# Conditioning sums taken one block of 512 at a time on TensorE or VectorE, with six half tiles instead of four

## The chip, the cores and the metric

The kernel runs on one core of a Trainium2 chip. The metric is the time of one launch on the device, in microseconds (us). A launch is one pass through a two-layer model with 256 latent tokens and 256 context tokens.

## The reference, cut to what matters

Each layer makes six vectors of 1024 values (shift, scale and gate, twice) from a conditioning vector and a 1024 x 6144 matrix. They are used wherever the layer is normalised or its result is added:

```
cond_lat = silu(c)                      # 1 x 1024
cond_ctx = silu(c_ctx)                  # 1024
for layer in range(2):
    sh1, sc1, g1, sh2, sc2, g2 = split(cond_lat @ ada_w[layer] + ada_b[layer], 6)
    h_l = rmsnorm(x, norm1_g[layer]) * (1 + sc1) + sh1
    if layer == 0:                      # the context rows need shift and scale once
        csh1, csc1, ... = split(cond_ctx @ ada_w[0] + ada_b[0], 6)
        y = hybrid_mix(h_c, h_l, ...)   # SSD heads and latent attention heads
    else:
        y = chunk_gmlp(h_l, ...)
    x = x + g1 * y
    x = x + g2 * peer(rmsnorm(x, norm2_g[layer]) * (1 + sc2) + sh2, ...)
return rmsnorm(x, final_norm_g)
```

So `cond @ ada_w` is a product of one row (two, where the context needs them) with 2 x 1024 x 6144 numbers of 4 bytes.

## The kernel before, in words

**Stages.** `hybrid` (layer 0's mixer) runs first, then `peer(0)`, `gmlp`, and `peer(1)`. In the profile `hybrid` lasts until about 440 us; its scheduled part, in which the change lies, until about 392 us.

**How the order is made.** The kernel keeps a model of the engines' clocks (`Clock`, `Engine`): every call to an engine (`T` for TensorE, `V` for VectorE, `S` for ScalarE, `G` for GpSimd, `Q` for the SP queue's transfers) adds an assumed cost to that engine's clock. `schedule` takes several generators (streams) and steps, each time, the one whose engine's clock is earliest, unless the condition it last yielded is not yet true. Out of this comes one fixed order of instructions per engine; on the chip every engine runs its own list in that order and waits on semaphores where data or a buffer is not there. All recorded operations carry line 173, the line of the helper that issues them, so that the tile names tell them apart. A matmul with an output of 32 partitions is assumed to cost 0.45 us, whatever stands next to it.

**The conditioning rows.** `ada_w` is cut into six groups of 2048 columns (two layers, three groups each); a group is four blocks of 512 sums. Layer 0's first group is made by `ada_first` and `second`, which the change leaves as they are. The other five, 20 blocks of 512 sums, are made by the stream `adas`, one after the other, through `ada_group`. In a group, block `t` (0 to 3) is accumulated over eight 128-row pieces `k` into the partitions 32t to 32t+31 of one PSUM bank. Each of the 160 pieces is a tile `aw` of 128 x 512 numbers (256 KB) that is loaded by the SP queue and then multiplied with `condT[:, k, :]` (128 x 32, of which two columns are not zero):

```
units = [(k, t) for k in range(KD) for t in range(4)]
mm(ps[32 * t:32 * t + 32, :], condT[:, k, :], bufs[i % n + j], k == 0, k == KD - 1)
```

`k` is the outer loop, `t` the inner, so that neighbouring matmuls write to different 32-partition column groups of the bank. Loads and matmuls go in pairs: a pair of tiles is loaded again when both have been used. There are four tiles (`NAW = 4`). When a group is complete, VectorE adds the bias to the whole bank (`ada_tail`).

**What stands beside it.** `adas` shares `schedule` first with the input products (`products`: tiles `whl`, `hh`, `hl`), the convolution (`conv`: `cacc`, `xch`), `dkv`, `decays`, `xtrans`, `cqs` and `states`, and then with the heads (`scores`: `kn`, `qn`, `krT`, `pe`; `values`: `pT`, `vt`; `segments`, `weights`, `outputs`: `seg`, `MT`, `yt`) and `joined` (`w_out`). The weights of those products are loaded by the same SP queue into four tiles `wr`, rounded by ScalarE into one half of three tiles `whl`, and the rest, their difference, is put by GpSimd (or VectorE) into the other half.

Of the kernel before, what the change touches and what calls it, by code (L numbers as in the profile page):

```python
# [17 lines left out]
ALU = mybir.AluOpType  # L18
AX = mybir.AxisListType

P = 128
D = 1024
KD = 8
# [26 lines left out]
EARLIER = 2.5  # L50
RUSH, SPREAD = 5.0, 2.6
PACE = 1.0
NAW = 4
KORDER = (8, 10, 12, 0, 2, 4, 6, 14)
LATE = 6.0
LAG = 2
# [151 lines left out]
def tile_backbone(ctx: ExitStack, tc: tile.TileContext, a: dict, out: bass.AP):  # L208
# [3 lines left out]
    clock = Clock()  # L212
    clk = clock.at
    T, V, S, G, Q = (Engine(e, n, clock) for e, n in ((nc.tensor, "T"), (nc.vector, "V"), (nc.scalar, "S"), (nc.gpsimd, "G"), (nc.sync, "D")))
# [28 lines left out]
    class Banks:  # L243
# [5 lines left out]
        def get(self):  # L249
            self.free.sort(key=clock.idle)  # L250
            return self.free.pop(0)
# [4 lines left out]
    def at(*aps):  # L256

        return lambda: clk["T"] + SLACK >= max(clock.ready(x) for x in aps)

    def mm(o, lhsT, rhs, start=True, stop=True):  # L260
        if rhs.dtype == F32 and lhsT.dtype == F32 and len(rhs.shape) == 2 and rhs.shape[1] == 512 and o.shape[0] == P:

            T.matmul(o[:, :256], lhsT, rhs[:, :256], start=start, stop=False)
            T.matmul(o[:, 256:], lhsT, rhs[:, 256:], start=False, stop=stop)
            return
        T.matmul(o, lhsT, rhs, start=start, stop=stop)
# [14 lines left out]
    ones = cp.tile([P, P], F32, name="ones")  # L281
# [24 lines left out]
    condT = cp.tile([P, KD, 32], F32, name="condT")  # L306
# [199 lines left out]
    def ada_tail(m, ps):  # L506
        V.tensor_tensor(m, ps, m, op=ALU.add)

    def ada_group(l, g, get, bufs, ps):

        units = [(k, t) for k in range(KD) for t in range(4)]
        n = len(bufs)
        for i in range(0, len(units) + n, 2):
            if i >= n:

                yield at(*bufs[i % n:i % n + 2])
                for j in range(2):
                    k, t = units[i - n + j]
                    mm(ps[32 * t:32 * t + 32, :], condT[:, k, :], bufs[i % n + j], k == 0, k == KD - 1)
            if i < len(units):  # L520
                yield lambda: clk["T"] >= max(clock.idle(x) for x in bufs[i % n:i % n + 2])
                for j in range(2):
                    k, t = units[i + j]
                    Q.dma_start(out=bufs[i % n + j], in_=a["ada_w"][l, k * P:(k + 1) * P, g * 2048 + t * 512:g * 2048 + (t + 1) * 512])
        ada_tail(get(), ps)
        yield

# [86 lines left out]
    def hybrid(mod):  # L614
# [87 lines left out]
        xw = e3.enter_context(tc.tile_pool(name="xw", bufs=1, side="right"))  # L702
        awb = [(ha if i < 3 else xw).tile([P, 512], F32, name=f"aw{i}") for i in range(NAW)]

# [39 lines left out]
        def adas():  # L744

            yield lambda: "mod1" in done
            ps = B.get()
            for l, g in ((0, 1), (0, 2), (1, 0), (1, 1), (1, 2)):
                if l == 0:
                    mod.append(mod_load(0, g))  # L750
                    yield from ada_group(l, g, lambda: mod[g], awb, ps)
                    done.add(("mod", g))
                    if g == 2:
                        mod2(0, mod, awb[0])
                elif g == 0:
                    yield from ada_group(l, g, lambda: nmod.append(mod_load(1, 0)) or nmod[0], awb, ps)
                else:
                    mt = ha.tile([P, 512], F32, name="mt", tag="mt")
                    yield from ada_group(l, g, lambda: mod_load(1, g, mt), awb, ps)
                    if g == 2:  # L760
                        mod2(1, [None, None, mt], awb[0])
                    S.dma_start(out=ms[g - 1], in_=mt)
            B.put(ps)
# [1410 lines left out]
```

## Time and profile before

| | |
|---|---|
| median of 3 runs | 1991.39 us (1984.33 to 1993.25) |
| the profiled execution: its time | 1996.46 us |
| the profiled execution: span of its instructions | 1994.7 us |
| mean granted TensorE clock in it | 0.97 of full speed |
| TensorE busy | 1863.6 us, 93% |
| VectorE busy | 1369.0 us, 69% |
| GpSimd busy | 629.5 us, 32% |
| ScalarE busy | 540.2 us, 27% |
| conditioning tiles loaded as `aw` | 164, of 256 KB each |

The page's busy time of TensorE counts the modelled run of each matmul through the array, and matmuls of one engine may overlap. A float32 matmul leaves two records in the trace, so that "x8" in a row on such matmuls means four of them. The idle time of an engine is given with what ended it. Of the rest of the page only what the rows below show is needed.

### The profile page before, as it was taken

What the parts mean: (1) busy time and instruction counts of PE and PEld (TensorE: products, weight loads), DVE (VectorE), ACT (ScalarE), POOL (GpSimd) and SP (SyncE); (2) the same over time, 40 slices, a digit from 0 to 9 for tenths busy, and PEclk for the clock granted to TensorE, in tenths of its full rate; (3) what the DMA queues carried; (4) which work ended last, traced back from release to release, by engine and by line L of the source; (5) the groups of instructions that cost most, each with busy time, mean ns of one, the idle gap of its engine ahead of it and who ended that gap; (6) DMA issues with size and microseconds to landing.
All of it is one profiled execution on the core that took longest, in us unless ns stands there. A gap on an engine that the chain in (4) does not pass through costs nothing. (4 is left out here: it accounts for less than half of the span.)

```text
span 1994.7 us, 27972 instructions
## 1 busy us (share of the span) xinstructions
PE 1863.6 (93%) x9888; PEld 1539.0 (77%) x9888; DVE 1369.0 (69%) x3376; ACT 540.2 (27%) x1428; POOL 629.5 (32%) x400
## 2 busy tenths in 40 slices
PE   7989999899999999998999698999999999989994
PEld 4666565679988878887878588799888888868773
DVE  4466276546985898778567625479858986876667
ACT  5334344345212222110111354442112221111111
POOL 2324312276010222133322198650112221334222
PEclk9999999899999999999999899999999999989998
DMA  8656766155367989699999474453579885999993
GB/s 314 217 173 220 251 219 212 68 180 169 128 218 276 358 301 365 221 359 367 398 417 395 149 254 147 161 188 128 195 286 362 302 342 220 355 355 400 417 411 128
DMA packets 133064, 529.87 MB, mean 266 GB/s; under 512 B 17941, under 2 KB 18133, under 8 KB 105197
## 3 DMA queue, kind: packets, MB, share of 16 engines
q1 hardware_dynamic: 97440, 301.76, 42.8%
q0 software_dynamic: 34176, 225.07, 28.9%
q8 instruction: 78, 1.28, 0.3%
q10 hardware_dynamic: 1296, 1.16, 0.2%
q14 instruction: 74, 0.61, 0.1%
HBM read 540.28 MB, written 6.91 MB: 274 GB/s over the span
## 5 line engine op out<-in xcount | busy, mean ns | idle before, releaser
L173 POOL DMA_INDIRECT rows<-in_uv,gidx x224 | 270.4, 1207 | 912.9 <-DVE acc L173 657.5
L173 PE MATMUL pb<-wr,ge 128*128 128x256 f32 x2400 | 539.5, 384 | 19.5 <-DMA wr<-in_dn 17.5
L173 PE MATMUL pa<-phf,wr 128*128 128x256 f32 x2400 | 539.1, 385 | 0.0
L173 PEld LDWEIGHTS pb<-wr,ge 128*128 128x128 f32 x2400 | 453.7, 191 | 103.1 <-DMA wr<-in_dn 41.9
L173 PEld LDWEIGHTS pa<-phf,wr 128*128 128x128 f32 x2400 | 458.9, 193 | 61.8
L173 POOL TENSOR_TENSOR whl<-wr,whl 128x1024 fp32r<-128x1024 f32 (+2 forms) x128 | 310.6, 2440 | 306.6 <-ACT whl L173 298.9
L173 DVE SCALAR_TENSOR_TENSOR junk<-rows,h 128x1024 bf16<-128x1024 f32 x224 | 273.8, 1222 | 128.7 <-DMA rows<-in_uv,gidx 128.6
L173 DVE SCALAR_TENSOR_TENSOR acc<-rows,wt,acc 128x1024 f32<-128x1024 f32 x220 | 281.8, 1281 | 0.3 <-ACT wt L173 0.3
L173 ACT ACTIVATE act<-act 128x1 f32<-128x1 f32 x230 | 46.7, 203 | 573.7 <-DVE junk L173 554.8
L173 ACT CAST whl<-wr 128x1024 fp32r<-128x1024 f32 (+2 forms) x136 | 137.3, 1019 | 86.3 <-PE pa L173 37.2
L173 ACT ACTIVATE sg<-pa 128x8 f32<-128x8 f32 (+20 forms) x98 | 26.5, 270 | 278.1 <-PE pa L173 252.3
L173 PE MATMUL pb<-oc,o 128*128 128x75 f16 x1024 | 85.3, 252 | 14.8 <-DVE oc L173 13.6
L173 PE MATMUL pa<-phh,whl 128*128 128x256 f32 x512 | 96.3, 285 | 2.2 <-DVE phf L173 1.5
L173 PEld LDWEIGHTS <-o 128*128 128x128 f16 x1024 | 78.0, 118 | 24.0 <-DVE oc L173 14.8
L173 ACT ACTIVATE ge<-pa 128x256 f32<-128x256 f32 (+18 forms) x146 | 46.9, 321 | 144.9 <-PE pa L173 144.3
L173 PE MATMUL pa<-aw,condT 128*32 128x512 f32 x320 | 78.7, 605 | 6.9 <-DMA aw<-in_ada_w 5.1
L173 PEld LDWEIGHTS pa<-phh,whl 128*128 128x128 f32 x512 | 80.7, 191 | 3.6 <-DVE phf L173 1.9
L173 DVE SCALAR_TENSOR_TENSOR ge<-pb,ge 128x292 f32<-128x292 f32 (+19 forms) x128 | 42.1, 370 | 59.4 <-ACT ge L173 56.5
L173 PE MATMUL pa<-phl,whl 128*128 128x256 f32 x256 | 73.2, 286 | 2.4 <-POOL phl L173 1.3
L173 DVE TENSOR_TENSOR o<-iotaJ,pkT 128x1024 f16<-128x1024 f16 x64 | 43.8, 684 | 36.8 <-PE pb L173 36.8
L173 ACT ACTIVATE wt<-act,gsel 128x1 f32<-128x1 f32 x224 | 66.0, 295 | 7.3
L173 DVE MAX8 ge<-ge 128x8 f32<-128x128 f32 (+1 forms) x192 | 38.4, 254 | 26.0 <-ACT ge L173 25.9
(490 smaller groups left out, 2436.6 us busy)
## 6 DMA issues: line engine op xcount, KB each, us to landing
wr<-in_dn SPq DMA_DIRECT2D x300, 512.0 KB
aw<-in_ada_w SPq DMA_DIRECT2D x164, 256.0 KB
wr<-in_wq SPq DMA_DIRECT2D x32, 512.0 KB
wr<-in_w_out SPq DMA_DIRECT2D x16, 512.0 KB
wr<-in_gm_w_v SPq DMA_DIRECT2D x16, 512.0 KB
wr<-in_gm_w_u SPq DMA_DIRECT2D x16, 512.0 KB
wr<-in_gm_w_out SPq DMA_DIRECT2D x16, 512.0 KB
wr<-in_w_xbc SPq DMA_DIRECT2D x12, 512.0 KB
```

Of the source, the lines that this page charges most:

```text
L173: return f(*args, **kw)
```

## The change

`ada_group` now takes the blocks one after the other: `t` is the outer loop, `k` the inner. Tiles are loaded and used singly, and there are six (`NAW = 6`). At the first piece of a block the model's clocks decide who makes it. If VectorE's clock is not past TensorE's, VectorE multiplies the tile by the conditioning value of its row (`tensor_scalar`, in place), and adds the next seven pieces to it (`scalar_tensor_tensor`), and one matmul with a matrix of ones sums the result over the partitions. Otherwise TensorE makes the block with eight matmuls as before.

```diff
-NAW = 4
+AHEAD = 0.0
+NAW = 6
...
     def ada_group(l, g, get, bufs, ps):
...
-        units = [(k, t) for k in range(KD) for t in range(4)]
-        n = len(bufs)
-        for i in range(0, len(units) + n, 2):
-            if i >= n:
-
-                yield at(*bufs[i % n:i % n + 2])
-                for j in range(2):
-                    k, t = units[i - n + j]
-                    mm(ps[32 * t:32 * t + 32, :], condT[:, k, :], bufs[i % n + j], k == 0, k == KD - 1)
-            if i < len(units):
-                yield lambda: clk["T"] >= max(clock.idle(x) for x in bufs[i % n:i % n + 2])
-                for j in range(2):
-                    k, t = units[i + j]
-                    Q.dma_start(out=bufs[i % n + j], in_=a["ada_w"][l, k * P:(k + 1) * P, g * 2048 + t * 512:g * 2048 + (t + 1) * 512])
+        units = [(t, k) for t in range(4) for k in range(KD)]
+        free, way, acc = list(bufs), [], None
+        while units or way:
+            while units and free:
+                free.sort(key=clock.idle)
+                aw = free.pop(0)
+                yield lambda: clk["T"] >= clock.idle(aw)
+                t, k = units.pop(0)
+                Q.dma_start(out=aw, in_=a["ada_w"][l, k * P:(k + 1) * P, g * 2048 + t * 512:g * 2048 + (t + 1) * 512])
+                way.append((t, k, aw))
+            t, k, aw = way.pop(0)
+            yield at(aw)
+            if k == 0:
+                acc = aw if clk["V"] <= clk["T"] + AHEAD else None
+            if acc is None:
+                mm(ps[32 * t:32 * t + 32, :], condT[:, k, :], aw, k == 0, k == KD - 1)
+                free.append(aw)
+                continue
+            if k == 0:
+                V.tensor_scalar(acc, aw, condT[:, k, 0:1], None, op0=ALU.mult)
+                continue
+            V.scalar_tensor_tensor(acc, aw, condT[:, k, 0:1], acc, op0=ALU.mult, op1=ALU.add)
+            free.append(aw)
+            if k == KD - 1:
+                yield lambda: clk["T"] >= clock.ready(acc) + 1.0
+                mm(ps[32 * t:32 * t + 32, :], ones[:, 0:32], acc)
+                free.append(acc)
         ada_tail(get(), ps)
         yield
```

In the order that comes out, 16 of the 20 blocks stay on TensorE (128 matmuls) and 4 go to VectorE (4 `TENSOR_SCALAR`, 28 `SCALAR_TENSOR_TENSOR`), with 4 matmuls with `ones`. Before, the 160 matmuls stood in 55 uninterrupted bursts, 30 of two and 25 of four; now the 132 stand in 38 bursts of one to six.

TensorE, at the first burst of `adas`, between the input products of `dkv` and of `xbc`. Before:

```order
L173 MATMUL pa_125<-whl_343,hl_394 128x336
L173 MATMUL pa_126<-aw0_310,condT_82 32x512
L173 MATMUL pa_126<-aw1_311,condT_82 32x512
L173 MATMUL pa_126<-aw2_312,condT_82 32x512
L173 MATMUL pa_126<-aw3_313,condT_82 32x512
L173 MATMUL pb_127<-hh_139,whl_409 128x512
```

and now:

```order
L174 MATMUL pa_125<-whl_345,hl_396 128x336
L174 MATMUL pa_126<-aw4_314,condT_82 32x512
L174 MATMUL pa_126<-aw5_315,condT_82 32x512
L174 MATMUL pa_126<-aw0_310,condT_82 32x512
L174 MATMUL pa_126<-aw1_311,condT_82 32x512
L174 MATMUL pa_126<-aw2_312,condT_82 32x512
L174 MATMUL pa_126<-aw3_313,condT_82 32x512
L174 MATMUL pb_127<-hh_139,whl_411 128x512
```

Before, the four matmuls are piece 0 of blocks 0 to 3 and write to four column groups; now the six are pieces 0 to 5 of block 0 and write to one.

VectorE at the same place, after the last `hl` of the modulation and ahead of `dkv`'s `dtx`. Before:

```order
L173 TENSOR_TENSOR hl_510<-hm_498,hh_139 128x512
L173 TENSOR_TENSOR dtx_320<-pb_129,c1_318 128x16 x2
L173 TENSOR_TENSOR dtx_320<-pb_130,c1_318 128x16 x2
L173 TENSOR_TENSOR dtx_320<-pa_124,c1_318 128x16 x2
L173 TENSOR_TENSOR dtx_320<-pa_125,c1_318 128x16 x2
```

and now:

```order
L174 TENSOR_TENSOR hl_515<-hm_502,hh_139 128x512
L174 TENSOR_SCALAR aw0_310<-aw0_310,condT_82 128x512
L174 SCALAR_TENSOR_TENSOR aw0_310<-aw1_311,condT_82,aw0_310 128x512
L174 SCALAR_TENSOR_TENSOR aw0_310<-aw2_312,condT_82,aw0_310 128x512
L174 SCALAR_TENSOR_TENSOR aw0_310<-aw3_313,condT_82,aw0_310 128x512
L174 SCALAR_TENSOR_TENSOR aw0_310<-aw4_314,condT_82,aw0_310 128x512
L174 SCALAR_TENSOR_TENSOR aw0_310<-aw5_315,condT_82,aw0_310 128x512
L174 SCALAR_TENSOR_TENSOR aw0_310<-aw1_311,condT_82,aw0_310 128x512
L174 SCALAR_TENSOR_TENSOR aw0_310<-aw2_312,condT_82,aw0_310 128x512
L174 TENSOR_TENSOR dtx_322<-pb_129,c1_320 128x16 x2
```

The eight new operations are block 1 of the group; each reads a tile that the SP queue loads, and `dtx` stands behind them.

TensorE, where that block is closed, now:

```order
L174 MATMUL pa_123<-hh_139,whl_570 128x512
L174 MATMUL pa_126<-aw0_310,ones_76 32x512
L174 MATMUL pa_126<-aw3_313,condT_82 32x512
L174 MATMUL pa_126<-aw4_314,condT_82 32x512
L174 MATMUL pa_126<-aw5_315,condT_82 32x512
L174 MATMUL pa_126<-aw1_311,condT_82 32x512
L174 MATMUL pa_126<-aw2_312,condT_82 32x512
L174 MATMUL pb_128<-ident_69,ckn_649 128x128 x2
```

One matmul with `ones` stands where eight would; the five behind it are pieces of block 2, in one column group again.

Two smaller moves come with it. The last conditioning matmul stood right ahead of the weights' products of the fourth and last pair of heads; now it stands ahead of those of the third pair. In `features` of `peer(0)` ten matmuls with `identb` now stand ahead of the product with `diag`; before there were none at that place.

## Rows read from the trace of the kernel before

**Rows 1.** The page's head: the span, and busy time of each engine.

```profile
span 1994.7 us, 27972 instructions
PE 1863.6 (93%) x9888; PEld 1539.0 (77%) x9888; DVE 1369.0 (69%) x3376; ACT 540.2 (27%) x1428; POOL 629.5 (32%) x400
```

**Rows 2.** Busy time by stretch; the columns stand in the first row.

```profile
core 0: us, PE busy (x) PEld busy (x) DVE busy (x) ACT busy (x) POOL busy (x), PEclk, DMA share, GB/s
0.00:38.00 38.00, 26.59 (x124) 12.68 (x126) 14.69 (x49) 20.15 (x41) 6.22 (x13) 1.00 0.95 348
38.00:350.00 312.00, 295.67 (x1440) 189.13 (x1440) 178.49 (x368) 123.16 (x224) 93.03 (x44) 0.98 0.65 215
350.00:392.00 42.00, 34.37 (x187) 27.29 (x185) 26.82 (x57) 16.38 (x34) 7.65 (x3) 0.91 0.17 62
195.00:226.00 31.00, 30.45 (x126) 17.28 (x125) 7.21 (x9) 8.60 (x11) 8.98 (x4) 1.00 0.72 232
500.00:700.00 200.00, 200.00 (x1106) 178.03 (x1106) 158.43 (x530) 44.23 (x155) 26.65 (x23) 1.00 0.68 246
```

**Rows 3.** Instructions by group: shapes, xrecords | busy us, mean ns | idle before.

```profile
L173 PE MATMUL pa<-aw,condT 128*32 128x512 f32 x320 | 78.7, 605 | 6.9 <-DMA aw<-in_ada_w 5.1 <-DVE mod L173 1.8
```

**Rows 4.** TensorE in order of time: start, us, what, xrecords.

```profile
20.27 1.05 PE L173 MATMUL pa<-zs,condT 128*32 128x512 f32 x4
...
22.28 1.91 PE L173 MATMUL pa<-wr,condT 128*32 128x512 f32 x8
...
33.10 1.04 PE L173 MATMUL pb<-aw,condT 128*32 128x512 f32 x2
34.08 0.58 PE L173 MATMUL pb<-whl,hh 128*128 128x336 f32 x2
...
47.14 1.07 PE L173 MATMUL pa<-aw,condT 128*32 128x512 f32 x8
48.14 0.50 PE L173 MATMUL pb<-hh,whl 128*128 128x512 f32 x1
```

**Rows 5.** The same view, a burst of four whose tiles came late.

```profile
58.80 2.29 PE L173 MATMUL pa<-aw,condT 128*32 128x512 f32 x6
62.23 1.04 PE L173 MATMUL pa<-aw,condT 128*32 128x512 f32 x2 [1.13 <-DMA aw<-in_ada_w]
63.21 0.58 PE L173 MATMUL pb<-whl,hh 128*128 128x336 f32 x2
```

**Rows 6.** What TensorE waited for, 40 to 392 us: total, times, longest.

```profile
PE pb L173 <- ACT xch L173: 6.3, 2, 3.4
...
PE pb L173 <- DVE pT L173: 2.6, 2, 2.1
...
PE pb L173 <- ACT yt L173: 2.6, 1, 2.6
PE pb L173 <- ACT krT L173: 2.0, 1, 2.0
```

**Rows 7.** VectorE's groups by shape, 38 to 392 us; columns as in rows 3.

```profile
L173 DVE SCALAR_TENSOR_TENSOR cacc<-xpad,c,cacc 128x512 f32<-128x512 f32 x40 | 30.1, 752 | 1.4
...
L173 DVE TENSOR_SCALAR cacc<-xpad,c 128x512 f32<-128x512 f32 x10 | 12.9, 1286 | 14.0 <-ACT xpad L173 13.9
...
L173 DVE TENSOR_SCALAR pe<-pe,sm 128x512 f32<-128x512 f32 x16 | 7.8, 487 | 0.6
```

**Rows 8.** What VectorE waited for, 44 to 70 us and 190 to 245 us.

```profile
DVE dtx L173 <- PE pb L173: 16.3, 2, 15.6
...
DVE kn L173 <- PE pa L173: 21.3, 1, 21.3
```

**Rows 9.** What the SP queue's issuing waited for, 40 to 350 us.

```profile
SPq L173 <- PE pa L173: 142.2, 66, 9.8
SPq L173 <- POOL whl L173: 48.9, 14, 8.6
```

**Rows 10.** Matmuls with `identb` in the whole run; TensorE at the first `features`.

```profile
L173 PE MATMUL pb<-ones,identb 128*128 128x256 f16 x34 | 4.0, 273 | 1.0 <-DVE x L173 1.0
...
444.57 2.71 PE L173 MATMUL pa<-diag,x 128*128 128x128 f32 x11 [1.73 <-DVE a L173]
```

## The prediction

> **What bounds the kernel now.** I read the page's head first: TensorE is busy 93% of the span, no other engine over 69% [rows 1]. Then busy time by stretch. Between 38 and 350 us, where `adas` runs, TensorE is busy 295.67 of 312 us, and in the experts' stage 200.00 of 200 [rows 2]. So in the stretch that the change touches, work taken from TensorE's list or put on it moves the end nearly one for one; the other engines have gaps. The list of waits says what fills the rest: 6.3 us for `xch`, 2.0 for `krT`, and small ones near the end of the heads [rows 6]. Then the group of conditioning matmuls: 320 records, 160 matmuls, 78.7 us with 6.9 us of waiting ahead of them, 85.6 us of TensorE's time [rows 3]. This is the sum that the change works on. Last, TensorE in order of time, to see what one such matmul costs alone and in company. That view decides.
>
> **What a matmul of 32 columns costs.** One alone, at 33.10, is followed by the next product 0.98 us later. Four, at 47.14, are followed 1.00 us later [rows 4]: those four write to four column groups, and run side by side. Two in two groups, at 20.27, take 1.05 us; four in the same two groups, at 22.28, take 1.91 [rows 4]. So a second matmul in a column group adds 0.86 us, and one in another group nothing. The planner assumes 0.45 us for each in either case, so it does not see the difference.
>
> A rule of the Trainium skill bears on mixed bursts: "TensorE: Matmul & The Clock Gate", Part 3 on packing small matmuls, says that matmuls start and end in program order. No row here shows a burst with several of one group ahead of another group. By that rule alone, the second piece of a block would hold up the next block behind it, nothing would overlap, and the time below would come out 6 us higher.
>
> **The change, term by term.** The sum is made against the profiled execution, 1996.46 us (span 1994.7); it lies 5 us over the median of 1991.39, so the difference is put on the median.
>
> *Blocks on TensorE.* 132 matmuls in 38 bursts. With `k` inside `t`, neighbours are in one group. A burst of n in one group costs n x 0.86 + 0.12 (0.98 for one). If nothing overlaps: 132 x 0.86 + 38 x 0.12 = 118.1 us. If, where a block ends inside a burst, the two groups run fully side by side, only the larger group of each burst counts, 119 matmuls in all: 106.9 us. I take the middle, 112.5, as no row is nearer to either.
>
> *Tiles that come late.* Before, 55 bursts at 0.98 (30 of two) or 1.00 (25 of four) would be 54.4 us; they take 85.6. The other 31 us are late tiles: at 58.80 three matmuls start as their tiles land and the fourth waits until 62.23, and the next product starts 4.41 us after the first [rows 5]. Now a burst of six holds TensorE for 5.3 us by itself, which is longer than that spread of 3.4 us, so mostly the first tile of a burst can still be waited for. The nearest row is the waiting shown as idle, 6.9 us [rows 3]; at 38 bursts instead of 55 that is 5 us. Ends: 0 and 15, half of what was lost. The fifth and sixth tile are in this term; otherwise they cost no time.
>
> Together 117.5 us in place of 85.6: **+32 us** (ends +21 and +48). Had the 28 matmuls only been taken away, at the old mean of 0.54 us (85.6/160), it would be -15. The loss of company costs three times what VectorE takes over.
>
> *VectorE.* 28 additions of 128 x 512 at 0.752 us and 4 scalings at between 0.487 and 1.286 [rows 7]: 23.0 to 26.2 us. They lie beside TensorE: one block falls where VectorE waited 16.3 us for `dkv`'s products, the other three around 195 to 226 us, where it is busy 7.21 of 31 us and waits 21.3 us in one piece for the first heads [rows 2, 8]. Cost 0. If that cover is gone, one block (6 us) shows; ends 0 and +6. A late tile also holds up what is queued behind it on VectorE, first `dtx` and then `conv`, for whose `xch` TensorE waits.
>
> *Waits that are taken up.* TensorE is now later against ScalarE and VectorE than the planner thinks. Of the 8.3 us for `xch` and `krT` [rows 6] I take half: -4 (ends -8 and 0).
>
> *The end of the heads.* The conditioning matmuls used to fill gaps between the score products; now the last two pairs of heads run without them, before it was one. In the stretch of the last pair TensorE is idle 7.6 of 42 us [rows 2], of which `pT` and `yt` are 5.2 [rows 6]. Not all comes twice, since the weights of the last pair can be multiplied in between: +2 (ends 0 and +7).
>
> *SP and the rest.* The SP queue issues the same 160 loads, now one by one, each held until its tile is free. It already stands 142.2 us waiting for TensorE's releases [rows 9], and the `wr` loads stand behind them. Four `wr` tiles and three `whl` lie between; I put 0 (end: the fourth case below). The ten `identb` matmuls take 10 x 0.12 us (4.0 over 34) and lie in a wait of 1.73 us for `diag` [rows 10]: 0. The experts' stages get no new work and only a few rows change places: 0, plus or minus 4.
>
> Sum: +32 - 4 + 2 = **+30 us, 2021 us** on the median.
>
> **The rivals.**
>
> 1. *Taken up elsewhere.* TensorE's added time falls where it would have waited anyway: tiles no longer late, `xch`, the heads' softmax. For it: late tiles are 31 us of the 85.6. Against: they are already counted above, and outside this group TensorE is idle only 17 us from 38 to 392 us (16.3 + 7.6 - 6.9) [rows 2, 3]. With the low end of every term, +21 - 8 = +13; it takes another few us of luck in the experts' stages to stay within 0.5%: about 1998 us.
>
> 2. *Faster.* Neighbours in one column group run into each other after all, so that a burst of six costs about what a burst of four does now. Place: the 38 bursts. Price: 38 x 1.00 + 5 = 43 us in place of 85.6, so -43, 1949 us; no change would be at (85.6 - 5 - 38 x 0.12)/132 = 0.58 us for a matmul, and it decides for faster, by 10 us, once one costs under 0.5. Against it: the 0.86 us of the burst at 22.28, whose tiles had landed [rows 4].
>
> 3. *The SP queue turns the delay over.* Each load waits for one matmul of a burst that is now twice as long as planned, or for VectorE, which itself waits for a tile. The next `wr` stands behind, and TensorE then waits for weights too. For it: the 142.2 us [rows 9], with single waits of up to 9.8 us. Against: no weight load is on TensorE's list of waits now. One such wait of 2 us in about every third burst is +25 more: 2046 us.
>
> **How the numbers follow.** The forecast, matmuls one after the other and the rest hidden, gets 0.70; taken up elsewhere 0.12, faster 0.06, SP 0.12. The likeliest gives 2021 us; its own bounds are +13 (low ends) to +48 + 2, 2004 to 2041. The range reaches down into the first rival and just into the third: 1996 to 2043; outside lie the faster case and about half of the first and third, under 0.2. A measurement of this kernel tells about 0.5% from no change, 10 us: under 1981 counts as faster, over 2001 as slower. Faster 0.06 is the second rival; same 0.12 is the first; slower 0.82 is the forecast and the third.
>
> **What the profile of the changed kernel would show.** The conditioning group with 256 records (and 8 for `ones`) and more busy time than before, 105 to 120 us; a burst of six about 5.3 us long, the starts of its matmuls 0.86 us apart; late tiles seldom. VectorE 23 to 26 us busier, with its blocks in former waits. TensorE busy over 97% between 38 us and the end of `adas`, and that end 25 to 40 us later. The experts' stages as long as before within 4 us. Wrong would be: matmuls of one group starting within a few ns of each other (second rival), `wr` or ScalarE's `whl` as what TensorE waits for (third), or the same end of `hybrid` with TensorE's idle time gone (first).

## The result, and the profile after

The changed kernel takes 2010.52 us (median of 4 runs, 2007.97 to 2012.38) against 1988.68 for the kernel before, measured beside it (4 runs, 1984.33 to 1993.25): 1.0104 times as long, 95% interval 1.0079 to 1.013. It is slower, by 21.8 us where +30 was forecast, and inside the range.

Each of the two kernels was profiled twice. In the pair of first profiles the spans are 1994.7 and 2007.6 us, in the second 1992.3 and 2009.0; the profiled executions of the kernel before lie 5 to 8 us over its median, those of the changed one on it, so the profiles show 12.9 and 16.7 of the 21.8 us, and what follows accounts for those.

The page's head and the conditioning groups of the changed kernel (page and groups by line; columns as in [rows 3]):

```profile
span 2007.6 us, 27950 instructions
PE 1891.0 (94%) x9842; PEld 1552.1 (77%) x9842; DVE 1401.9 (70%) x3410; ACT 545.1 (27%) x1431; POOL 627.7 (31%) x398
...
L174 PE MATMUL pa<-aw,condT 128*32 128x512 f32 x256 | 107.3, 596 | 1.4 <-DVE mod L174 1.4
...
L174 PE MATMUL pa<-aw,ones 128*32 128x512 f32 x8 | 4.2, 604 | 1.6 <-DVE aw L174 1.6
...
L174 DVE SCALAR_TENSOR_TENSOR aw<-aw,condT,aw 128x512 f32<-128x512 f32 x28 | 27.4, 978 | 12.8 <-DMA aw<-in_ada_w 12.2
...
L174 DVE TENSOR_SCALAR aw<-aw,condT 128x512 f32<-128x512 f32 x4 | 5.6, 1392 | 3.1 <-DMA aw<-in_ada_w 3.1
```

Fewer products (256 records instead of 320) take more of TensorE: 107.3 us where it was 78.7 [rows 3]. The wait for late tiles, 5.1 of the 6.9 us there, is gone from this group: now it is VectorE that waits for tiles, 15.3 us, in its own former gaps. VectorE's busy time rose by 32.9 us [rows 1], which is these 33.0.

TensorE in order of time, changed kernel, two bursts of six (start, us, what, xrecords):

```profile
46.04 5.34 PE L174 MATMUL pa<-aw,condT 128*32 128x512 f32 x12
51.31 0.51 PE L174 MATMUL pb<-hh,whl 128*128 128x512 f32 x1
...
81.32 3.63 PE L174 MATMUL pa<-aw,condT 128*32 128x512 f32 x12
84.88 0.33 PE L174 MATMUL pa<-ident,xch 128*128 128x128 f32 x1
```

The first six are all of one block: the next product starts 5.27 us later, which is 6 x 0.86 + 0.11. The second six are the last two of one block and the first four of the next: 3.56 us, which is 4 x 0.86 + 0.12. So the two blocks run side by side in full, and only the larger group of a burst counts.

What TensorE waited for, changed kernel, 40 to 392 us (total, times, longest), to hold against [rows 6], and busy time by stretch, to hold against [rows 2] (columns as there):

```profile
PE pb L174 <- ACT pe L174: 3.8, 3, 2.7
PE pa L174 <- ACT pe L174: 3.4, 2, 1.7
PE pa L174 <- ACT kn L174: 2.7, 1, 2.7
PE pa L174 <- DVE mod L174: 2.2, 2, 1.4
PE pa L174 <- DVE aw L174: 1.6, 1, 1.6
```

```profile
38.00:350.00 312.00, 302.45 (x1274) 182.31 (x1273) 197.13 (x365) 112.78 (x200) 87.87 (x40) 0.99 0.64 211
350.00:392.00 42.00, 34.44 (x198) 28.33 (x197) 31.86 (x69) 17.23 (x32) 9.34 (x4) 0.92 0.22 78
195.00:226.00 31.00, 27.90 (x113) 18.60 (x112) 28.03 (x29) 14.04 (x24) 17.09 (x6) 1.00 0.57 192
500.00:700.00 200.00, 200.00 (x1143) 179.96 (x1142) 159.05 (x597) 49.86 (x150) 36.51 (x25) 1.00 0.64 227
```

`xch` and `krT` are no longer waited for; `pe` and `kn`, of the heads, stand in their place. VectorE is busy 28.03 of the 31 us around 210, where it was 7.21: the blocks went where the prediction put them. The first `diag` product, which begins the first features, stood at 444.57 us [rows 10]; now it stands at

```profile
464.02 2.27 PE L174 MATMUL pa<-diag,x 128*128 128x128 f32 x9 [2.88 <-DVE a L174]
```

(TensorE in order of time), 19.5 us later. From there to the end of the span it is 1550.2 us before and 1543.6 after. So the time was lost ahead of the first features, and the following stages gave 6.6 us back in this pair.

### The profile page after: what moved, and what is told of

Same layout as the page of the kernel before. It is cut to its first block, busy times and chain, and to the rows that moved or that the text cites. A ratio compares the mean times of both kernels' runs of the same rounds, so it can differ in the third digit from the quotient of the medians.

```text
span 2007.6 us, 27950 instructions
## 1 busy us (share of the span) xinstructions
PE 1891.0 (94%) x9842; PEld 1552.1 (77%) x9842; DVE 1401.9 (70%) x3410; ACT 545.1 (27%) x1431; POOL 627.7 (31%) x398
## 5 line engine op out<-in xcount | busy, mean ns | idle before, releaser
L174 PE MATMUL pb<-wr,ge 128*128 128x256 f32 x2400 | 541.1, 386 | 15.0 <-DMA wr<-in_dn 13.1
L174 PE MATMUL pa<-aw,condT 128*32 128x512 f32 x256 | 107.3, 596 | 1.4 <-DVE mod L174 1.4
L174 ACT ACTIVATE sg<-pa 128x8 f32<-128x8 f32 (+23 forms) x98 | 26.4, 270 | 277.4 <-PE pa L174 248.6
L174 PE MATMUL pb<-oc,o 128*128 128x75 f16 x1024 | 84.9, 252 | 11.7 <-DVE oc L174 10.7
L174 ACT ACTIVATE ge<-pa 128x256 f32<-128x256 f32 (+22 forms) x146 | 46.9, 321 | 144.9 <-PE pa L174 144.3
L174 DVE SCALAR_TENSOR_TENSOR ge<-pb,ge 128x196 f32<-128x196 f32 (+19 forms) x128 | 41.9, 368 | 60.5 <-ACT ge L174 60.0
L174 PE MATMUL pb<-whl,cath 128*128 128x512 f32 x224 | 71.8, 399 | 2.0 <-POOL whl L174 1.1
L174 PEld LDWEIGHTS pa<-aw,condT 128*32 128x32 f32 x256 | 23.1, 109 | 62.1 <-issue 58.7
```

What stands on the lines that cost most here:

```text
L174: return f(*args, **kw)
```

## How the first half is accounted for

These figures are read from each trace, all on TensorE between 40 us and the first `diag` product. **By group:** what the bursts would take at 0.86 us per product of the largest column group in each, plus 0.12 per burst. **Conditioning path:** for each burst of the conditioning products of `adas` the time from its start to the start of the next other product, with the idle time just ahead of it, summed; what the path has beyond the price by group are late tiles, waits, and bursts that ran at half clock. **Other idle:** TensorE's idle time outside the path. **Half clock:** the time in which the clock was granted at 1.2 instead of 2.4 GHz. **Lost to it:** half of that time, as far as TensorE worked in it and outside the path, for work done in it takes about twice as long. The fours paced at 8 us (below) show this on one burst of four at half clock and one after it, each with the product that follows (TensorE in order of time): 1.86 us to the next product in the first, 0.99 in the second.

```profile
243.73 1.94 PE L174 MATMUL pa<-aw,condT 128*32 128x512 f32 x8
245.59 0.80 PE L174 MATMUL pb<-ckh,whl 128*128 128x512 f32 x1
...
251.96 1.06 PE L174 MATMUL pa<-aw,condT 128*32 128x512 f32 x8
252.95 0.44 PE L174 MATMUL pb<-ident,pe 128*128 128x128 f32 x2
```

| kernel | by group | path | other idle | half clock | lost to it | first features | median us | ratio to before (95%) |
|---|---|---|---|---|---|---|---|---|
| before, two profiles | 53.9 | 84.7, 85.2 | 17.9, 18.2 | 29.6, 32.8 | 12.8, 13.0 | 444.6, 446.0 | 1988.7 | |
| changed, two profiles | 106.9 | 109.7, 109.7 | 17.8, 16.7 | 17.1, 14.4 | 7.4, 6.2 | 464.0, 462.6 | 2010.5 | 1.0104 (1.0079 to 1.013) |
| one by one, all TensorE | 120.0 | 130.5 | 28.5 | 35.1 | 10.0 | 498.8 | 2050.3 | 1.0299 (1.0271 to 1.0328) |
| side by side, six tiles | 55.5 | 95.3 | 27.0 | 48.9 | 12.0 | 464.2 | 2013.2 | 1.011 (1.0084 to 1.0137) |
| the same, with VectorE | 58.8 | 88.8 | 32.1 | 54.6 | 14.4 | 466.1 | 2005.6 | 1.0077 (1.0052 to 1.0103) |
| fours, seven tiles | 39.2 | 61.5 | 31.8 | 50.3 | 16.5 | 438.1 | 1987.7 | 0.9983 (0.9966 to 1.0) |
| changed, four tiles | 88.3 | 106.6 | 39.3 | 60.7 | 12.9 | 488.5 | 2044.7 | 1.028 (1.0247 to 1.0313) |
| before, six tiles | 51.2 | 73.3 | 27.4 | 31.1 | 11.1 | 441.9 | 2007.2 | 1.0092 (1.007 to 1.0114) |
| fours, four tiles | 39.2 | 78.8 | 25.0 | 38.3 | 11.9 | 443.2 | 1995.8 | 1.003 (1.0016 to 1.0045) |
| fours, every 7 us | 39.2 | 54.1 | 35.6 | 41.0 | 14.9 | 434.3 | 1985.5 | 0.9977 (0.9962 to 0.9992) |
| fours, every 8 us | 39.2 | 53.6 | 24.4 | 47.8 | 19.1 | 425.2 | 1976.3 | 0.9929 (0.9901 to 0.9957) |
| fours, every 9 us | 39.2 | 57.6 | 30.5 | 34.3 | 13.1 | 429.8 | 1992.6 | 1.0032 (1.001 to 1.0055) |

Path, other idle and what was lost to the clock, taken from the time of the first features, leave between 327.5 and 330.9 us in all 14 profiles: these three terms account for the first half. In the kernels after the first two, what comes behind the first features lasts 1538 to 1563 us, without any of the edits being there; so a median alone says less of the conditioning than the time of the first features does.

## The experiments

The theory tested (A): a product's price on TensorE is set by what stands beside it in its burst, 0.86 us in the same column group and almost nothing in another. Rivals: the conditioning that ends early leaves the first half's last heads without work to fill their waits (C); tiles come late because too few are free (D); those waits and the half clock have another cause than lacking filler (E).

**One by one, all on TensorE.** The changed kernel without VectorE's part; tiles and order as changed.

```diff
-                acc = aw if clk["V"] <= clk["T"] + AHEAD else None
+                acc = None
```

> The changed kernel with no block on VectorE: all 160 conditioning matmuls on TensorE, block after block, six tiles. Theory A (the matmuls lost their company: each in the same 32-partition column group adds 0.86 us): 40 bursts whose larger groups add up to about 120 us of TensorE's time in place of 107, so about 12 us slower than the changed kernel and 33 us slower than before (ratio 1.017). Theory B (VectorE's blocks, held up by late tiles, and the SP queue's single loads cost the 22 us): no slower than the changed kernel, up to 20 us faster.

Measured 2050.3 us. TensorE's group and its longest wait (groups by line; waits, 38 to 500 us):

```profile
L174 PE MATMUL pa<-aw,condT 128*32 128x512 f32 x320 | 129.7, 602 | 3.5 <-DVE mod L174 3.5
...
PE pb L174 <- ACT pe L174: 12.5, 2, 11.0
```

The same 320 records as before take 129.7 instead of 78.7 us. The run is 39.8 us slower than the changed kernel: theory B, by which it would be no slower, fell, and A has the direction but only 12 of the 39.8 us. In the profiles the four blocks on VectorE are worth 20.7 us on the path, 10.7 of other idle time and 2.6 of clock, 34.0 of the 34.7 us between the first features. So VectorE's share is a gain of 40 us; the rest of the change (the order, single loads and six tiles together) costs 59 (1.0299 times the time before), and the next run takes the order out of it.

**Side by side, six tiles.** That kernel with the loops turned round: same tiles, single loads, no VectorE.

```diff
-        units = [(t, k) for t in range(4) for k in range(KD)]
+        units = [(k, t) for k in range(KD) for t in range(4)]
...
+                acc = None
```

> The same as the run before it but with k as the outer loop, t as the inner: neighbouring matmuls in four column groups again, six tiles, loaded singly, nothing on VectorE. Theory A: 56 us of TensorE's time if all tiles are in time, 56 to 80 with late ones, against 85 before: 5 to 30 us faster than before (ratio 0.985 to 0.997), 40 to 60 us faster than the series on TensorE alone. Theory B: the order of the matmuls makes no difference, so within 5 us of the series on TensorE alone.

Measured 2013.2 us: the order alone is worth 37.1 us (A expected 40 to 60, B under 5), and the path is 35.1 us shorter. Company's price is shown. But A also had this kernel 5 to 30 us faster than the one before, and it is 1.1% slower, though it has the same order of loops. Its group says where half of that lies (groups by line):

```profile
L174 PE MATMUL pa<-aw,condT 128*32 128x512 f32 x320 | 80.1, 632 | 17.2 <-DMA aw<-in_ada_w 10.3 <-DVE mod L174 6.9
```

By group it would be 55.5 us, the path is 95.3: 40 us of late tiles, waits and half clock, where one by one 10.5 were left. Products that run four at a time use up six tiles in one and a half bursts. Against the kernel before the path is 10.6 us longer, and other idle time 9.1.

**The same, with VectorE.** The fourth block of a group goes to VectorE where it is free (2 of 20 blocks).

```diff
+                accs[t] = aw if t == 3 and clk["V"] <= clk["T"] + AHEAD else None
+            acc = accs[t]
```

> Side by side with six tiles as in the second run, but the fourth block of a group goes to VectorE where the model has it free (2 of 20 blocks; 146 matmuls on TensorE). Theory A: a burst of three takes as long as one of four, so VectorE's help is worth nothing: 59 us plus late tiles, within 6 us of the second run on either side. Theory B: VectorE's blocks cost: more than 6 us slower than the second run. A third idea, that each matmul taken from TensorE saves its share, would make it 7 us faster than the second run.

Measured 2005.6 us, 7.5 less. That is the third idea's number, and just outside A's 6 us, but it does not come from the first half: the first features come 1.9 us later (466.1), and the rest of the kernel is 8.0 us shorter. The path is 6.6 us shorter, though by group it is 3.3 us longer, so less of it is waiting; 5.1 us more of other idle time and 2.4 more lost to the clock took that back. Three products side by side last as long as four, 0.99 us to the next product (TensorE in order of time):

```profile
209.89 1.06 PE L174 MATMUL pa<-aw,condT 128*32 128x512 f32 x6
210.88 0.48 PE L174 MATMUL pb<-xw,xctx 128*128 128x256 f32 x1
```

**Fours, seven tiles.** Always four products of one `k`, in four groups, all on TensorE; seven tiles.

```diff
-NAW = 6
+NAW = 7
...
-            t, k, aw = way.pop(0)
-            yield at(aw)
+            four = [way.pop(0) for _ in range(4)]
+            yield at(*[aw for _, _, aw in four])
+            for t, k, aw in four:
```

> All on TensorE, always four matmuls of one k in four column groups, seven tiles (the most that fit). Theory A: 40 bursts at 1.00 us, 40 us if the tiles are in time, up to 65 with late ones: 15 to 45 us faster than before (ratio 0.977 to 0.992). Theory B: seven tiles and no VectorE block, so no worse than before, but the bursts of four give nothing over the pairs: ratio 0.995 to 1.005.

Measured 1987.7 us, the time of the kernel before: B's number, and A's 15 to 45 us did not come. But the path did fall, by 23 us (61.5, within A's 65), so B's reason is not the cause; the first features fell only by 6.5, since 13.9 us more idle elsewhere and 3.7 more lost to the clock took most of it.

**Changed, four tiles.** The changed kernel with `NAW = 4`; by the planner's clocks eight blocks then go to VectorE.

> The changed kernel with four half tiles instead of six and nothing else: the order then gives eight of the twenty blocks to VectorE (64 products there, 104 products with 32 columns left on TensorE after the head, in 41 bursts). Theory A (what a product costs TensorE is set by its column group): the bursts come to 88.3 us at 0.86 us per product in the busiest group, 18.6 less than the changed kernel's 106.9, so about 1992 us, 1.000 to 1.004 of the kernel before; VectorE busy 60 to 66 us on it instead of 33, hidden. Theory D (six tiles are needed once the sums run block by block, since one of four is held by VectorE's sum): leads of late tiles above 12 us and about 2005 or more.

Measured 2044.7 us: theory A's 1992 fell. D's "about 2005 or more" covers the time, but not its sign: TensorE itself waited 0.7 us for late tiles. Against the changed kernel the path is 3.1 us shorter, and other idle time 21.5 longer. VectorE's groups, what VectorE waited for (38 to 500 us), and the last two sums in TensorE's order of time:

```profile
L174 DVE SCALAR_TENSOR_TENSOR aw<-aw,condT,aw 128x512 f32<-128x512 f32 x56 | 66.4, 1186 | 11.5 <-DMA aw<-in_ada_w 11.0
...
DVE aw L174 <- DMA aw<-in_ada_w: 32.3, 15, 11.6
...
463.96 1.04 PE L174 MATMUL pa<-aw,ones 128*32 128x512 f32 x2 [2.08 <-DVE aw L174]
476.34 1.92 PE L174 MATMUL pa<-aw,ones 128*32 128x512 f32 x2 [3.99 <-DVE aw L174]
```

VectorE no longer hides its part: 74.5 us of blocks with 32.3 us of waiting for tiles, the last of them finished at 476 us, and the first features wait for them, at 488.5. In the changed kernel VectorE's last block was done by 257 us. That VectorE hides its part holds for four blocks with six tiles, and not for eight with four.

**Before, six tiles.** The kernel before with `NAW = 6`.

> The kernel before with six half tiles and nothing else (pairs of column groups as before, 160 products on TensorE after the head, 40 bursts with 51.2 us at the price by column group, against 53.9 before). Theory A: conditioning 2 to 3 us shorter or, with tiles in time, up to 25 us shorter (before spent 84.7 us on it, 31 of them beyond the price by group), so 1965 to 1989. Theory C (what is saved ahead of the first half's last heads comes back as waits and half clock there, because the conditioning ends earlier): conditioning path under 75 us and yet 1985 to 1995, last conditioning product before 330 us, over 35 us at half clock ahead of the first features.

The path is 73.3 us (11.4 less), between A's two cases, but the first features come only 2.7 us earlier (441.9): 9.5 us more of other idle time took most of it back. That is what C says, and the last conditioning product stands at 274.3 us, ahead of C's 330; C's half clock of over 35 us did not come (31.1). The median, 2007.2 us, fits neither theory, because the last part of the second layer's experts became longer: from the last `wr,ge` product to the end it is 53.9 us, before 38.5. TensorE's waits from 500 us on say where, first this kernel, then the kernel before:

```profile
PE pb L173 <- DVE sc L173: 37.4, 4, 22.6
```

```profile
PE pb L173 <- DVE sc L173: 19.1, 2, 10.9
```

The planner hands out the experts' rows by its clocks, so an edit in the first half can move them too. The run paced at 9 us has the same long end (51.9 us). That the planner's clocks are the cause is argued, and was not tried.

**Fours, four tiles.** The fours with `NAW = 4`.

> The kernel's half tiles as before (four), but loaded and multiplied four at a time, side by side, all on TensorE, without a pace: the order alone of the kernel before is changed. Price by column group 39.2 us. If tiles in time need more than four of them (Theory D): TensorE waits for the tiles inside its bursts as in the kernel before, conditioning 75 us or more, 1985 to 2000. If company alone sets it (Theory A) the conditioning takes about 60 us and the kernel 1970 to 1980. The last conditioning products come in the order behind the first products of the output projection, so features that wait for them would add 10 us or more.

Theory D holds, and A's 1970 to 1980 fell: path 78.8 us and 1995.8. In the groups by line, this one first, then the run with seven tiles:

```profile
L174 PE MATMUL pa<-aw,condT 128*32 128x512 f32 x320 | 65.3, 616 | 7.7 <-DMA aw<-in_ada_w 7.7
```

```profile
L174 PE MATMUL pa<-aw,condT 128*32 128x512 f32 x320 | 55.1, 619 | 6.0 <-DMA aw<-in_ada_w 5.9
```

Company is worth its price only where the tiles are there.

**Fours, paced.** The run with seven tiles, and at most one four every 7, 8 or 9 us of the planner's clock.

```diff
+            yield lambda: clk["T"] >= due[0]
+            due[0] = max(due[0], clk["T"] - 7.0) + 8.0
```

> The four side by side with seven tiles, all on TensorE, as in the run of fours, but with one group of four at most every 7 us of the order's own clock, so that the conditioning lasts through the first half's heads. Price by column group the same, 39.2 us. Theory C (early end leaves the heads without filler, and the clock falls): fewer waits and less half clock between 300 and 440 us than the run of fours (which had 50.3 us at half clock ahead of the first features), conditioning path still about 60 us or less, and 1965 to 1980. Rival E (waits of the heads and the half clock come from elsewhere and not from the lack of filler): as the run of fours, 1983 to 1992.

> As the run paced at 7 us, at 8 us: the last conditioning products come near the end of the first half. Theory C: no worse than the run paced at 7 us, 1960 to 1980; if the last group of sums comes so late that the first features wait for it, 1985 or more. Rival E: 1983 to 1992.

> As the run paced at 8 us, at 9 us: the last conditioning products come in the order behind the first products of the output projection, so this looks at the far edge. Conditioning path 50 to 56 us. If nothing waits for the last sums 1970 to 1980 (about as at 8 us); if the first features wait for them, 1980 to 1995, with a wait for ACT pe or DVE mod of over 5 us.

At 7 us 1985.5, at 8 us 1976.3, at 9 us 1992.6. The run at 8 us beats both kernels: 0.9929 times the time before (0.9901 to 0.9957), 34 us under the changed one. Its group, by line, has the tiles in time:

```profile
L174 PE MATMUL pa<-aw,condT 128*32 128x512 f32 x320 | 48.7, 640 | 0.2 <-DMA aw<-in_ada_w 0.2
```

Neither C nor E holds whole. The last conditioning product moved from 308.6 us without a pace to 330.0 and 366.7, through the heads. At 7 us the time is in E's range, and between 300 and 440 us TensorE idled 18.2 us, with 23.9 at half clock, where it was 16.7 and 21.4 without a pace. At 8 us the time is in C's range and under E's, and the idle time there fell to 11.5 us, but the half clock rose to 27.3. Against the run without a pace the first features at 8 us come 12.9 us earlier: 7.9 on the path, as the pace leaves time for the loads, and 7.4 of other idle time, against 2.6 more lost to the clock. At 9 us that turns (path 57.6, over the 50 to 56 expected, with 4.5 us of waiting for tiles; other idle 30.5), and the long end named above comes on top. What sets the idle time elsewhere was not tried, so 8 us is a pace that was found, one of three, and not one that was derived.

**Both kernels again.** No edit; only the half clock was asked for.

> The changed kernel itself, profiled a second time, to see whether the half clock ahead of the first features (17.1 us in its first profile) is a trait of the kernel or of one execution. If of the kernel: 14 to 20 us again and the first features at 463 to 466 us. If of the execution: 24 us or more, and features 3 us later or more.

> The kernel before itself, profiled a second time (its first profile was 1996.46 us, above its median). Half clock ahead of the first features 29.6 us in the first profile. If that is a trait of the kernel: 27 to 33 us again and the first features at 443 to 446 us. If of the execution: under 24 us, features at 441 us or earlier, and then the changed kernel's first half is more than 20 us behind.

14.4 us for the changed kernel (17.1 at first), 32.8 for the kernel before (29.6): as far as two profiles can show, a trait of each kernel and not of an execution. The first features stand within 1.4 us of the first profiles.

## Why the prediction was right, and where it was not

- **The loss of company.** Right in cause: without VectorE's part the change costs 59 us against the kernel before, and the order of the loops alone wins 37.1 of them back. The step "costs three times what VectorE takes over" is mis-sized: VectorE's part is worth 39.8 us, so it is one and a half times. The 28 products were priced there at their old mean of 0.54 us (-15); one by one they cost 0.86, and the path is 20.7 us shorter without them, the rest is mostly other idle time.
- **Blocks on TensorE, 112.5 us.** Mis-sized: this is the step "I take the middle". The bursts measure 106.7 us in the changed kernel's first profile, at the low end, 106.9. Blocks that meet in a burst overlap in full. The rule of the Trainium skill ("TensorE: Matmul & The Clock Gate", Part 3 on packing small matmuls), that matmuls start in program order, does not describe these rows: in the burst at 81.32 the second matmul of the first block would have to start ahead of the second block, and the six would take 5 x 0.86 + 0.12 = 4.42 us (5.28 in the prediction's stricter reading); they take 3.56.
- **Late tiles, 5 us.** None: the 3.0 us of the path ahead of the bursts are the waits for `mod` (1.4) and for one of VectorE's sums (1.6). Path 109.7 against the 117.5 forecast, before 84.7 against 85.6: +25.0 instead of +32 (+24.6 in the second profiles).
- **VectorE, 23.0 to 26.2 us, hidden.** 33.0 us, and hidden: TensorE waited 1.6 us for one sum. The price per addition, 0.752 us from [rows 7], was right for 24 of 28; the other four, and two of the four scalings, took 1.5 to 2.8 us (below).
- **Waits taken up, -4, and the heads' end, +2.** Other idle time went from 17.9 to 17.8 us, 18.2 to 16.7 in the second profiles: -0.1 and -1.5 for both together, where -2 was forecast. That the sum is near is luck: the 8.3 us for `xch` and `krT` are gone whole, not by half, and 9.9 us for `pe` and `kn` came in their place.
- **What was not in the sum: the clock.** 12.5 us less at the half clock in the first pair, 18.4 in the second, which gave back 5.4 and 6.8 us. Path, waits and clock make +19.5 us in the first pair (25.0 - 0.1 - 5.4) and +16.3 in the second (24.6 - 1.5 - 6.8); the first features are 19.5 and 16.6 us later, so no further term is needed.
- **The experts' stages, 0 plus or minus 4.** -6.6 us in the first pair, +0.1 in the second; over all kernels 1538 to 1563 us. The bound was too narrow for a planner that orders these stages by the clocks of what comes before.
- **Signs named in advance.** Right: 256 and 8 records, 105 to 120 us (107.3), 5.3 us for six of one block. Missed: VectorE is 33.0 us busier, not 23 to 26; TensorE is busy 302.45 of the 312 us up to 350, 96.9%, not over 97; and the last conditioning product comes 5.1 us earlier (341.4 for 346.5), not 25 to 40 later. One by one the blocks stand earlier in the order; the delay shows in the input products, whose last stands at 246.1 instead of 224.3 us.
- **The rivals.** Faster fell with the 5.27 us burst. The SP queue fell: its waits for TensorE's releases of `pa`, 142.2 us in [rows 9], are now 124.4, the longest 6.3 instead of 9.8; those for VectorE's tiles come to 13.8; and TensorE's list has no wait for `wr` or `whl` (SP's waits, 40 to 350 us):

```profile
SPq L174 <- PE pa L174: 124.4, 96, 6.3
...
SPq L174 <- DVE aw L174: 13.8, 12, 4.0
```

  Taken up elsewhere is true in small part, by the clock (5.4 and 6.8 us) more than by waits (0.1 and 1.5).

The forecast lay 8 us high: 7 us too many for the path and 5 to 7 for the clock, against which stand the 5 to 9 us by which the pairs of profiles differ less than the medians. So 5 to 9 of the 21.8 us lie outside what the profiles show.

## What to carry to other kernels

Where small matmuls fill only part of the array's columns, their price is that of the busiest column group in a burst: order them so that neighbours go to different groups, and let the planner's cost say so, before moving any to another engine. Then the loads become the limit, so give the fours enough tiles and a pace; here that, at one pace of three, and not the split with VectorE, beat the tuned kernel. Judge an early edit by a landmark behind it as well as by the total, when a planner orders the later stages by the same clocks.

## What was not expected of the hardware

**The clock fell where TensorE had gaps.** Busy time by stretch, kernel before and then the changed kernel; the granted clock is the first figure behind the engines:

```profile
80.00:120.00 40.00, 35.09 (x169) 23.42 (x166) 26.38 (x47) 14.75 (x31) 12.78 (x7) 0.93 0.62 205
120.00:160.00 40.00, 36.60 (x169) 25.17 (x168) 26.29 (x44) 15.65 (x27) 10.79 (x5) 0.94 0.45 141
```

```profile
80.00:120.00 40.00, 40.00 (x169) 22.79 (x169) 26.70 (x50) 14.54 (x31) 10.09 (x6) 1.00 0.64 211
120.00:160.00 40.00, 40.00 (x146) 21.84 (x145) 17.15 (x37) 15.70 (x24) 11.17 (x5) 1.00 0.59 188
```

Where TensorE had idle gaps it was granted 0.93 and 0.94 of full speed, with stretches at 1.2 GHz in them; without gaps 2.4 GHz throughout. Work taken off TensorE can come back as half clock: the fours paced at 8 us, with 31 us less of conditioning, spent 47.8 us at half clock, 15 to 18 more than before. The sum of the gaps does not settle it: ahead of the first features TensorE idled 31.7 us in all there, and 42.1 us with 34.3 at half clock when paced at 9 us. Which gaps count was not tried.

**VectorE's additions and scalings wait for GpSimd.** Changed kernel, order of time, VectorE and then GpSimd:

```profile
198.40 2.57 DVE L174 TENSOR_SCALAR aw<-aw,condT 128x512 f32<-128x512 f32 x1
201.01 2.33 DVE L174 SCALAR_TENSOR_TENSOR aw<-aw,condT,aw 128x512 f32<-128x512 f32 x3
```

```profile
194.56 6.13 POOL L174 TENSOR_TENSOR whl<-wr,whl 128x1024 fp32r<-128x1024 f32 x2 [5.94 <-ACT whl L174]
```

The scaling at 198.40 begins while GpSimd makes a `whl` (until 200.69) and ends 0.28 us behind it, after 2.57 us; the next three, with GpSimd idle, take 0.75 us each. All six long ones of the 32 (1.5 to 2.8 us) begin so beside a running `whl` of GpSimd, and none clear of one took more than 0.75; nor did those that began shortly ahead of a `whl`. This agrees with what the Trainium skill says in "Trainium Architecture — The Big Picture", section "What this means for kernel authors", of a port that VectorE and GpSimd share by an exclusive lock.
